# One decoder block on one core: the conditioning vector's load, the first rounded operand, r from PSUM, and the planner's clock

## Chip, core and metric

The kernel runs on one core of one Trainium2 chip. The time is device time of one execution in microseconds, the median of several runs. The profile is of one execution, with its own time.

## What is computed

One decoder block on x (1,024 tokens by 1,024 channels, float32), with a conditioning vector c:

```python
c_act = silu(c)
shift1, scale1, gate1, shift2, scale2, gate2 = split(c_act @ ada_w + ada_b, 6)
h = rmsnorm(x, norm1_g) * (1 + scale1) + shift1
u, v, val, gate = split(h @ w_in + b_in)           # 512 channels each
y_a = gelu(u) * (causal 128x128 mixing of layernorm(gelu(v)) per head)
y_b = silu(groupnorm(causal conv31(val * sigmoid(gate))))
x = x + gate1 * (concat(rmsnorm(y_a), rmsnorm(y_b)) @ w_out)
h2 = rmsnorm(x, norm2_g) * (1 + scale2) + shift2
g, up = split(h2 @ w_ffn_in)                        # 2816 channels each
x = x + gate2 * ((silu(g) * up) @ w_ffn_out)
out = rmsnorm(x, norm_f_g) * (1 + scale_f) + shift_f
```

## The kernel before

The data lie transposed: 128 channels on the partitions, tokens along the free dimension, eight tiles x0 to x7 of 128 x 1024. Tokens are worked in two halves of 512. Every large product is made of three matmuls (`mm3`, `product`): an operand is split into a rounded part (`hi`, type fp32r) and a remainder (`lo`), and hi by hi, lo by hi and hi by lo are summed in PSUM.

The start, which the change touches, goes so. `c_row` (L518) is loaded into one partition, two matmuls against a row of ones (L538) spread it over all partitions into two PSUM banks, and ScalarE's Silu gives `cact` (L539). The eight first halves of x are loaded (L524), squared on ScalarE (L641), and summed over channels by small fp32 matmuls (L648) into a bank; ScalarE takes the square root (L651), VectorE the reciprocal (L652), and matmuls with a selecting column out of the table `colt` (L654) spread the result r over the partitions of the same bank. With `copy=True` ScalarE then copies r into SBUF (L660). The bank is the only one of its tag (`nrm`); later it serves as one of the eight banks of the first projection.

Then a loop over the eight channel blocks k (L718). Two tiles of `ada` (128 x 1024) are loaded per block and multiplied with `cact` on VectorE with a sum over the row (L559), which gives the shift and scale columns (`ccol`); they land in `ypad` tiles, four in turn. A weight block `wk[k]` is loaded, its rounded part is made by ScalarE (L586) and its remainder by VectorE (L587). The block of x is multiplied by r on VectorE (L725), scaled and shifted by ScalarE in place (L726), rounded by ScalarE (L728), and the remainder is taken by VectorE (L729). Then come 24 matmuls of 512 columns into eight banks (L603 to L605). `gain` and the columns of biases come from `colt` (L521), one table of 277 columns.

Most of the order is not that of the program text. The text is emitted once, and `fix_order` (L452) then plans it: `Graph` collects instructions with what each must follow, `forward` is a list schedule over five engines in which `duration` gives each instruction a time and `Clock` keeps when an engine, the port shared by VectorE and GpSimd and the load queue come free, and `backward` gives each instruction the time from it to the end, which is its rank in the next `forward`. After three rounds the plan with the smallest planned end is kept, and its order on every engine, SyncE's loads too, is written into the program. `issue_after(ins)` adds the demand that what is issued on the same engine in its block comes after `ins`. In the plan before, six loads of x stand ahead of the load of c.

Of the kernel before, what the change touches and what calls it, by code (L numbers as in the profile page):

```python
# [15 lines left out]
D = 1024  # L16
# [51 lines left out]
DMA_ISSUE = 0.44  # L68
DMA_AHEAD = 0.5


# [53 lines left out]
def duration(s):  # L125
# [3 lines left out]
    if s.engine == "PE":  # L129
        n, m = s.writes[0].width, s.reads[1].width  # L130
        if not s.reads[0].f32:
            t = n / 512 * 0.2267
        elif n == 128:
            t = {128: 0.219, 32: 0.068}.get(m, 0.109)
        else:
            t = 0.857
        return t, t + 0.176, 0
# [34 lines left out]
class Graph:  # L172


    def __init__(self, instructions, edges, stacked, reusing):
        self.steps = []
        uses, live, tiles, order = {}, {}, {}, {}
        for ins in instructions:
# [3 lines left out]
            for operands, written in ((s.reads, False), (s.writes, True)):  # L182
                for o in operands:
# [17 lines left out]
                    if o.tile.tag and o.space != "DRAM" and o.name not in s.slots:  # L201
                        s.slots.append(o.name)
            self.steps.append(s)
        by_name = {s.ins.name: s for s in self.steps}
# [108 lines left out]
class Clock:  # L313


    def __init__(self):
        self.free = dict.fromkeys(ENGINES, 0.0)
        self.port = self.queue = 0.0
        self.last, self.partial = None, False

    def run(self, s, t):
        if s.dma:
            gap = (TURN_GAP if self.last is False else LOAD_GAP) if s.load else STORE_GAP if self.last else 0.0
            begin = max(t + (LOAD_WAIT if s.load else STORE_WAIT), self.queue + gap)
            self.queue = begin + s.bytes / (LOAD_RATE if s.load else STORE_RATE)
            self.last = s.load
            self.free["SP"] = max(t + DMA_ISSUE, self.queue - LOAD_WAIT - DMA_AHEAD)
            return t, self.queue
        if s.port:
            t = max(t, self.port)  # L330
            self.port = t + s.port
        if s.engine == "PE" and s.partial != self.partial:
            self.partial = s.partial
            t += 0.09 if s.partial else 0.12
        self.free[s.engine] = t + s.issue
        return t, t + s.finish
# [18 lines left out]
def forward(g, rank):  # L355
# [6 lines left out]
    parked = {tag: [] for tag in g.order}  # L362
    slots, clock, table = Slots(g), Clock(), None

# [16 lines left out]
    for _ in range(count):  # L381
# [21 lines left out]
        for n in s.after:  # L403
            need[n] -= 1
            same = g.steps[n].engine == e and not s.dma
            at[n] = max(at[n], (begin + s.issue if e == "PE" else end) if same else end + SIGNAL[e])
            if not need[n]:
                arrive(n)
# [60 lines left out]
def block_kernel(ctx: ExitStack, tc: tile.TileContext, xT, c, ada, cols, vbias, bs, wsp,  # L469
# [48 lines left out]
    c_row = sb.tile([P, D], F32, tag="raw", name="c_row", bufs=N_RAW)  # L518
    nc.sync.dma_start(c_row[0:1, :], c)
    colt = const.tile([P, NCOL], F32, name="colt")  # L520
    nc.sync.dma_start(colt, cols)  # L521
    xs = [const.tile([P, S], F32, name=f"x{k}") for k in range(KD)]
    for k in range(KD):
        nc.sync.dma_start(xs[k][:, hs(0)], xT[k, :, hs(0)])  # L524

# [105 lines left out]
    def rstd(srcs, n, name, groups, add_eng, copy=False, size=H, tmp=tmp, bank=None):  # L631
# [28 lines left out]
        A.activation(r, bank, AF.Copy)  # L660
        return r

# [47 lines left out]

    r1a = rstd(x_half(0), D, "n1_0", (1,) * 8, None, True)
    h1 = [[None] * KD, [None] * KD]
# [5 lines left out]
    for k in range(KD):  # L718
# [5 lines left out]
        t = tmp(f"t_h1_0_{k}")  # L724
        V.tensor_tensor(t, xs[k][:, hs(0)], r1a, op=ALU.mult)  # L725
        A.activation(t, t, AF.Identity, bias=ccol(SHIFT1, k), scale=ccol(SCALE1, k))  # L726
        h = h1[0][k] = act_tile(f"h1_0_{k}", 0)
        A.activation(h[:, 0, :], t, AF.Copy)  # L728
        V.tensor_tensor(h[:, 1, :], t, h[:, 0, :].bitcast(F32), op=ALU.subtract)  # L729
# [686 lines left out]
```

## Time and profile before

| | |
|---|---|
| median of 3 runs | 996.74 us (996.4 to 1000.49) |
| profiled execution | 996.41 us, span 994.4 us |
| mean granted TensorE clock | 0.995 |
| TensorE, VectorE, ScalarE, GpSimd busy | 97%, 86%, 48%, 39% |

The span runs from the first to the last instruction of the profiled execution; the rest of its time lies around it. The busy share of TensorE counts modelled ends of pipelined matmuls, so where its pace is wanted the number of matmuls in a stretch is the better reading.

### The profile page before, as it was taken

What the parts mean: (1) busy time and instruction counts of PE and PEld (TensorE: products, weight loads), DVE (VectorE), ACT (ScalarE), POOL (GpSimd) and SP (SyncE); (2) the same over time, 40 slices, a digit from 0 to 9 for tenths busy, and PEclk for the clock granted to TensorE, in tenths of its full rate; (3) what the DMA queues carried; (4) which work ended last, traced back from release to release, by engine and by line L of the source; (5) the groups of instructions that cost most, each with busy time, mean ns of one, the idle gap of its engine ahead of it and who ended that gap; (6) DMA issues with size and microseconds to landing.
All of it is one profiled execution on the core that took longest, in us unless ns stands there. A gap on an engine that the chain in (4) does not pass through costs nothing.

```text
span 994.4 us, 13218 instructions
## 1 busy us (share of the span) xinstructions
PE 961.9 (97%) x4645; PEld 773.6 (78%) x4645; DVE 855.2 (86%) x1197; ACT 474.0 (48%) x751; POOL 391.4 (39%) x232
## 2 busy tenths in 40 slices
PE   4999999999999999999999999999999999999994
PEld 2887777778878778888888877888887888888873
DVE  3969999999999444799999999998678989869946
ACT  6668467643484363564332332323337437236416
POOL 0037879755556111574445544445443100000121
PEclk9999999999999999999999999999999999999997
DMA  8983351524465515764677777677557838315104
GB/s 301 329 315 101 123 175 56 189 96 127 148 223 180 190 43 169 259 232 145 221 253 233 244 240 255 227 241 234 186 180 259 303 131 259 121 40 173 33 1 169
DMA packets 73667, 184.08 MB, mean 185 GB/s; under 512 B 8193, under 2 KB 10497, under 8 KB 73602
## 3 DMA queue, kind: packets, MB, share of 16 engines
q1 hardware_dynamic: 73602, 183.25, 55.6%
q8 instruction: 36, 0.59, 0.3%
q14 instruction: 29, 0.24, 0.1%
HBM read 142.06 MB, written 41.16 MB: 184 GB/s over the span
## 4 chain that ended last, share of the span: by engine, by line
PE 83%; DVE 10%; issue 2%; ACT 2%; DMA 1%; POOL 0%; SPq 0%; ACTq 0%; DVEq 0%; POOLq 0%
PE B L928 24%; PE C L928 14%; PE ah L928 11%; PE p L603 3%; PE po L603 3%; PE po L604 3%; PE po L605 3%; PE p L604 3%; PE p L605 3%; PE A L928 3%; DVE w_f L921 2%; PE v L604 2%; PE v L603 1%; PE pu L605 1%; PE v L605 1%
## 5 line engine op out<-in xcount | busy, mean ns | idle before, releaser
L928 PE MATMUL B<-h,w_f 128*128 128x512 f32 x816 | 190.8, 390 | 2.3 <-ACT x L1145 1.2
L928 PEld LDWEIGHTS B<-h,w_f 128*128 128x128 f32 x816 | 152.7, 188 | 36.4 <-DVE x L1147 3.1
L866 DVE SCALAR_TENSOR_TENSOR cv<-ypad,colt,cv 128x512 f32<-128x512 f32 x216 | 147.6, 745 | 0.5
L928 PE MATMUL B<-fa,w_d 128*128 128x512 f32 x528 | 125.5, 390 | 0.3 <-DVE x L1277 0.2
L928 PE MATMUL C<-h,w_f 128*128 128x512 f32 x528 | 123.6, 389 | 0.0
L928 PEld LDWEIGHTS B<-fa,w_d 128*128 128x128 f32 x528 | 98.8, 188 | 22.0 <-DVE x L1277 1.1
L928 PEld LDWEIGHTS C<-h,w_f 128*128 128x128 f32 x528 | 99.1, 188 | 20.6
L928 PE MATMUL ah<-h,wh_a 128*128 128x512 f32 x320 | 101.6, 395 | 0.5 <-ACT sg L673 0.5
L1209 POOL TENSOR_TENSOR sq_nf<-sq_nf,sq_nf 128x512 f32<-128x512 f32 x9 | 12.5, 1388 | 175.6 <-ACT sq_nf L1204 175.6
L920 ACT ACTIVATE w_d<-raw_d 128x512 fp32r<-128x512 f32 (+1 forms) x72 | 42.0, 593 | 83.0 <-PE B L928 34.0
L1170 POOL TENSOR_TENSOR x<-x,up 128x512 f32<-128x512 f32 x20 | 34.7, 1737 | 106.1 <-ACT x L1169 106.1
L587 POOL TENSOR_TENSOR wl_a<-raw_a,wh_a 128x1024 fp32r<-128x1024 f32 x20 | 49.2, 2461 | 67.8 <-ACT wh_a L586 57.7
L920 ACT ACTIVATE w_f<-raw_f 128x512 fp32r<-128x512 f32 x68 | 42.3, 627 | 68.4 <-PE B L928 41.6
L921 DVE TENSOR_TENSOR w_f<-raw_f,w_f 128x512 fp32r<-128x512 f32 x68 | 68.7, 1017 | 5.1 <-ACT w_f L920 5.0
L928 PEld LDWEIGHTS ah<-h,wh_a 128*128 128x128 f32 x320 | 59.9, 188 | 15.1 <-issue 1.4
L928 PE MATMUL C<-fa,w_d 128*128 128x512 f32 (+1 forms) x273 | 64.4, 384 | 0.0
L928 PE MATMUL ah<-h,wl_a 128*128 128x512 f32 x160 | 62.2, 390 | 0.0
L928 PEld LDWEIGHTS C<-fa,w_d 128*128 128x128 f32 x273 | 49.9, 188 | 11.0 <-issue 0.8
L921 DVE TENSOR_TENSOR fa<-a,fa 128x512 fp32r<-128x512 f32 x77 | 54.2, 743 | 1.7 <-ACT fa L920 1.7
L1277 DVE SCALAR_TENSOR_TENSOR x<-B,cond,x 128x512 f32<-128x512 f32 x48 | 35.6, 743 | 19.8 <-PE B L928 19.8
L920 ACT ACTIVATE fa<-a 128x512 fp32r<-128x512 f32 x77 | 46.0, 626 | 8.8 <-DMA a<-acts 5.7
L921 DVE TENSOR_TENSOR w_d<-raw_d,w_d 128x512 fp32r<-128x512 f32 (+1 forms) x72 | 47.8, 673 | 1.4 <-ACT w_d L920 1.4
(236 smaller groups left out, 2094.2 us busy)
## 6 DMA issues: line engine op xcount, KB each, us to landing
acts<-x SPq DMA_DIRECT2D x77, 256.0 KB, 3.1
a<-acts SPq DMA_DIRECT2D x77, 256.0 KB, 4.0
raw_f<-wf SPq DMA_DIRECT2D x32, 512.0 KB, 4.5
ada<-ada SPq DMA_DIRECT2D x24, 512.0 KB, 3.4
x<-ada SPq DMA_DIRECT2D x24, 512.0 KB, 3.8
raw_a<-wf SPq DMA_DIRECT2D x20, 512.0 KB, 3.8
ahead<-ahead SPq DMA_DIRECT2D x40, 256.0 KB, 3.0
ypad<-ada SPq DMA_DIRECT2D x16, 512.0 KB, 5.4
```

The lines of the kernel that those rows point to most:

```text
L587: lo_eng.tensor_tensor(lo, raw, hi.bitcast(F32), op=ALU.subtract)
L603: PE.matmul(acc, shi, mhi, start=start, stop=False)
L604: PE.matmul(acc, slo, mhi, start=False, stop=False)
L605: PE.matmul(acc, shi, mlo, start=False, stop=stop)
L866: V.scalar_tensor_tensor(accs[j], src, wc, accs[j], op0=ALU.mult, op1=ALU.add)
L920: A.activation(dst[:, 0, :], src, AF.Copy)
L921: lo_eng.tensor_tensor(dst[:, 1, :], src, dst[:, 0, :].bitcast(F32), op=ALU.subtract)
L928: last_mm = PE.matmul(bank[:, cols], s, m[:, cols], start=first and p == 0 and i == 0, stop=p == n - 1 and i == 2, skip_group_check=True)
L1170: G.tensor_tensor(g0, g0, up0, op=ALU.mult)
L1209: G.tensor_tensor(sums[half], sums[half], t, op=ALU.add)
L1277: V.scalar_tensor_tensor(xs[k][:, part], bank[:, cols], ccol(GATE2, k), xs[k][:, part], op0=ALU.mult, op1=ALU.add)
```

## The change

Four things are changed. The load of c is issued first; the eight loads of x and the load of `colt` must follow it, and `colt` now stands behind x in the text. In the loop over blocks, the rounded operand is made by one ScalarE pass (scale, shift and rounding at once) out of the product with r, and the unrounded value by a second pass over the same product. Block 0 is multiplied by r out of the PSUM bank, the other seven out of the copy. In the planner, small fp32 matmuls get other times, TensorE's writes to one bank keep their order in the text, and the forward plan doubles a matmul's time where the engine was little used shortly before (`tensor`, `throttled`).

```diff
--- before.py
+++ after.py
@@ -67,6 +67,7 @@
 LOAD_GAP, STORE_GAP, TURN_GAP = 0.07, 0.24, 0.3
 DMA_ISSUE = 0.44
 DMA_AHEAD = 0.5
+CLOCK_WINDOW = 3.4133
 
 
 class Step:
@@ -130,10 +131,9 @@
         n, m = s.writes[0].width, s.reads[1].width
         if not s.reads[0].f32:
             t = n / 512 * 0.2267
-        elif n == 128:
-            t = {128: 0.219, 32: 0.068}.get(m, 0.109)
         else:
-            t = 0.857
+            k = s.reads[0].box[1] - s.reads[0].box[0]
+            t = {128: 0.219, 32: 0.068}.get(m, 0.109 if k > 64 else 0.055) * n / 128
         return t, t + 0.176, 0
     if s.engine == "Activation":
         psum = any(o.space == "PSUM" for o in s.reads)
@@ -174,7 +174,7 @@
 
     def __init__(self, instructions, edges, stacked, reusing):
         self.steps = []
-        uses, live, tiles, order = {}, {}, {}, {}
+        uses, live, tiles, order, bank = {}, {}, {}, {}, {}
         for ins in instructions:
             if not type(ins).__name__.startswith("Inst"):
                 continue
@@ -200,6 +200,10 @@
                         uses[o.name].append(s.n)
                     if o.tile.tag and o.space != "DRAM" and o.name not in s.slots:
                         s.slots.append(o.name)
+            if s.engine == "PE":
+                if s.writes[0].name in bank:
+                    s.before.add(bank[s.writes[0].name])
+                bank[s.writes[0].name] = s.n
             self.steps.append(s)
         by_name = {s.ins.name: s for s in self.steps}
         for later, earlier in edges:
@@ -313,10 +317,28 @@
 class Clock:
 
 
-    def __init__(self):
+    def __init__(self, throttled=False):
         self.free = dict.fromkeys(ENGINES, 0.0)
         self.port = self.queue = 0.0
         self.last, self.partial = None, False
+        self.throttled, self.active = throttled, {}
+
+    def tensor(self, t, s):
+
+        if s.partial != self.partial:
+            self.partial = s.partial
+            t += 0.09 if s.partial else 0.12
+        w = int(t / CLOCK_WINDOW)
+        slow = 2 if self.throttled and self.active.get(w - 1, 0.0) < CLOCK_WINDOW / 2 else 1
+        end = t + slow * s.issue
+        a = t
+        while a < end:
+            w = int(a / CLOCK_WINDOW + 1e-9)
+            b = min(end, (w + 1) * CLOCK_WINDOW)
+            self.active[w] = self.active.get(w, 0.0) + b - a
+            a = b
+        self.free["PE"] = end
+        return t, t + slow * s.finish
 
     def run(self, s, t):
         if s.dma:
@@ -329,9 +351,8 @@
         if s.port:
             t = max(t, self.port)
             self.port = t + s.port
-        if s.engine == "PE" and s.partial != self.partial:
-            self.partial = s.partial
-            t += 0.09 if s.partial else 0.12
+        if s.engine == "PE":
+            return self.tensor(t, s)
         self.free[s.engine] = t + s.issue
         return t, t + s.finish
 
@@ -360,7 +381,7 @@
     done, order = [0.0] * count, {e: [] for e in ENGINES}
     ready, waiting = ({e: [] for e in ENGINES} for _ in range(2))
     parked = {tag: [] for tag in g.order}
-    slots, clock, table = Slots(g), Clock(), None
+    slots, clock, table = Slots(g), Clock(True), None
 
     def arrive(n):
         tag, t = slots.blocked_on(g.steps[n])
@@ -403,7 +424,7 @@
         for n in s.after:
             need[n] -= 1
             same = g.steps[n].engine == e and not s.dma
-            at[n] = max(at[n], (begin + s.issue if e == "PE" else end) if same else end + SIGNAL[e])
+            at[n] = max(at[n], (clock.free[e] if e == "PE" else end) if same else end + SIGNAL[e])
             if not need[n]:
                 arrive(n)
     return order, done, slots.follows
@@ -516,12 +537,13 @@
         return slice(half * H, (half + 1) * H)
 
     c_row = sb.tile([P, D], F32, tag="raw", name="c_row", bufs=N_RAW)
-    nc.sync.dma_start(c_row[0:1, :], c)
+    c_load = nc.sync.dma_start(c_row[0:1, :], c).ins
     colt = const.tile([P, NCOL], F32, name="colt")
-    nc.sync.dma_start(colt, cols)
     xs = [const.tile([P, S], F32, name=f"x{k}") for k in range(KD)]
-    for k in range(KD):
-        nc.sync.dma_start(xs[k][:, hs(0)], xT[k, :, hs(0)])
+    with issue_after(c_load):
+        for k in range(KD):
+            nc.sync.dma_start(xs[k][:, hs(0)], xT[k, :, hs(0)])
+        nc.sync.dma_start(colt, cols)
 
     def col(name, i=0):
         o = _OFF[name] + i
@@ -658,7 +680,7 @@
             return bank[:, 0:size]
         r = front.tile([P, H], F32, tag="s", name=f"r_{name}", bufs=4)
         A.activation(r, bank, AF.Copy)
-        return r
+        return bank[:, 0:size], r
 
     def x_half(half):
         return [xs[k][:, hs(half)] for k in range(KD)]
@@ -708,7 +730,7 @@
                                        col("a_ln_b", hp)[rows], bst[rows, hp, :],
                                        op0=ALU.mult, op1=ALU.add)
 
-    r1a = rstd(x_half(0), D, "n1_0", (1,) * 8, None, True)
+    r1a_bank, r1a = rstd(x_half(0), D, "n1_0", (1,) * 8, None, True)
     h1 = [[None] * KD, [None] * KD]
     alloc = [cv_bank] * 2 + [gn_bank] * 2 + [mm_bank] * 3 + [nrm_bank]
     acc = {(j, vg): alloc[2 * j + vg](f"p{j}_{vg}") for j in range(4) for vg in range(2)}
@@ -722,10 +744,10 @@
         A.activation(ccol(SCALE1, k), ccol(SCALE1, k), AF.Identity, bias=gain[:, k:k + 1], scale=col("norm1_g", k))
         A.activation(ccol(SHIFT1, k), ccol(SHIFT1, k), AF.Identity, bias=bcol(SHIFT1, k))
         t = tmp(f"t_h1_0_{k}")
-        V.tensor_tensor(t, xs[k][:, hs(0)], r1a, op=ALU.mult)
+        V.tensor_tensor(t, xs[k][:, hs(0)], r1a_bank if k == 0 else r1a, op=ALU.mult)
+        h = h1[0][k] = act_tile(f"h1_0_{k}", 0)
+        A.activation(h[:, 0, :], t, AF.Identity, bias=ccol(SHIFT1, k), scale=ccol(SCALE1, k))
         A.activation(t, t, AF.Identity, bias=ccol(SHIFT1, k), scale=ccol(SCALE1, k))
-        h = h1[0][k] = act_tile(f"h1_0_{k}", 0)
-        A.activation(h[:, 0, :], t, AF.Copy)
         V.tensor_tensor(h[:, 1, :], t, h[:, 0, :].bitcast(F32), op=ALU.subtract)
         for j in range(4):
             for vg in range(2):
```

## Rows read from the trace of the kernel before

**Rows 1.** The page: engines, busy us, share of the span, instructions.
```profile
PE 961.9 (97%) x4645; PEld 773.6 (78%) x4645; DVE 855.2 (86%) x1197; ACT 474.0 (48%) x751; POOL 391.4 (39%) x232
```

**Rows 2.** Waits of TensorE, 28 to 970 us: total, times, longest; six rows.
```profile
PE po L603 <- ACT y_b L824: 1.5, 1, 1.5
...
PE B L928 <- DVE x L1277: 0.2, 1, 0.2
```

**Rows 3.** Chain of waits over the start: start us, us, what.
```profile
9.87 2.00 PE c L538 x2
...
15.13 1.90 DVE ypad L559 x3
...
21.89 0.81 ACT t_h L726
22.71 0.95 ACT wh_k L586
23.65 0.53 ACT h L728
...
24.22 0.80 PE p L603
25.02 0.43 PE p L604
...
27.98 0.24 PE p L603
```

**Rows 4.** Timeline, 0 to 32 us: start us, us, what, idle before.
```profile
3.60 0.33 SPq L519 DMA_DIRECT2D c_row<-c  x1
...
10.61 1.28 ACT L539 ACT_TABLE_LOAD   x1
...
10.90 0.17 DVE L716 SCALAR_TENSOR_TENSOR gain<-colt 128x8 f32<-128x8 f32 x1 [9.94 <-DMA colt<-cols]
...
11.91 0.60 ACT L539 ACTIVATE cact<-c 128x512 f32<-128x512 f32 x1
...
12.40 0.62 ACT L641 ACTIVATE sq_n<-x 128x512 f32<-128x512 f32 x1
...
16.61 0.35 ACT L651 ACTIVATE rt_n<-ssq_n,epst 128x128 f32<-128x128 f32 x1
...
17.43 0.95 DVE L652 RECIPROCAL rt_n<-rt_n 128x128 f32<-128x128 f32 x1
...
18.43 2.08 PE L654 MATMUL ssq_n<-rt_n,colt 128*128 128x128 f32 x8 [2.95 <-DVE rt_n L652]
...
20.54 0.60 ACT L660 ACTIVATE r_n<-ssq_n 128x512 f32<-128x512 f32 x1 [1.76 <-PE ssq_n L654]
```

**Rows 5.** Windows: busy us (PE, PEld, DVE, ACT, POOL), clock, DMA share, GB/s.
```profile
0.00:9.40 9.40, 2.79 (x36) 0.99 (x40) 0.09 (x2) 4.54 (x7) 0.49 (x8) 1.00 0.71 238
0.00:10.80 10.80, 4.19 (x41) 1.51 (x42) 0.09 (x2) 5.88 (x9) 0.49 (x8) 1.00 0.75 259
...
0.00:13.40 13.40, 6.79 (x51) 2.21 (x52) 0.26 (x3) 8.09 (x11) 0.49 (x8) 1.00 0.80 288
```

**Rows 6.** VectorE's lines by form, 0 to 280 us: busy us, mean ns.
```profile
L725 DVE TENSOR_TENSOR t_h<-x,r_n 128x512 f32<-128x512 f32 x8 | 5.4, 685 | 0.0
...
L904 DVE TENSOR_TENSOR s<-s,gn 128x512 f32<-128x512 f32 x4 | 2.7, 684 | 0.6 <-PE gn L901 0.6
```

**Rows 7.** Timeline of VectorE, 33 to 39 us.
```profile
33.47 1.22 DVE L587 TENSOR_TENSOR wl_k<-raw_k,wh_k 128x1024 fp32r<-128x1024 f32 x1
34.61 1.22 DVE L559 SCALAR_TENSOR_TENSOR ypad<-ypad,cact 128x1024 f32<-128x1024 f32 x1
...
38.10 1.22 DVE L587 TENSOR_TENSOR wl_k<-raw_k,wh_k 128x1024 fp32r<-128x1024 f32 x1
```

**Rows 8.** Windows of the feed-forward pass; columns as in rows 5.
```profile
460.00:540.00 80.00, 80.00 (x354) 66.26 (x353) 79.58 (x107) 29.59 (x49) 35.70 (x21) 1.00 0.70 229
540.00:620.00 80.00, 78.93 (x343) 63.72 (x342) 79.98 (x101) 23.94 (x40) 40.20 (x24) 1.00 0.77 248
```

## The prediction

> **What bounds the kernel now.** I read the page first: TensorE is busy for 97% of the span, VectorE for 86%, nothing else for more than half [rows 1]. A busy share says nothing of where an edit of the first microseconds lands, so I asked next what TensorE waits for after its first projection has begun. Between 28 and 970 us it waits six times, 4.9 us in all [rows 2]. The reader is to see that from there on the kernel is one long stream of matmuls: whatever brings the start of that stream forward should come out at the end, unless another engine then falls behind.
>
> The chain of waits over the start shows what holds that start back [rows 3]. The first projection matmul runs at 24.22. Going back from it: the rounding pass of the first operand (23.65), a weight copy that stood ahead of it on ScalarE (22.71), the scale and shift pass (21.89), VectorE's products with the conditioning vector (15.13), and the two matmuls that spread that vector over the partitions (the first at 9.87, 2.00 us). The timeline has the engines' own order [rows 4]: SyncE issues the vector's load at 3.60, behind six loads of x; the eighth square starts only at 12.40, behind the Silu table and the first half of the activated vector; the square root comes at 16.61, the reciprocal at 17.43. So the chain that sets the start runs through c, and c is late by the place of its load, not by its size.
>
> **What the loads allow.** Counting bytes from time 0, 238 GB/s over 9.4 us are 2,237 KB: c (4), the eight halves of x (262 each) and the columns (142). To 10.8 us it is 2,797 KB, one conditioning tile (524) more; to 13.4 us 3,859 KB, which is both tiles and the first weight block [rows 5]. The gain product, which waited for the columns, starts at 10.90 [rows 4], so a load may be used up to 1.5 us after its bytes have passed. VectorE's first product at 15.13 therefore had its tile from about 11 or 12 on, and was waiting for c alone.
>
> **Edit 1, c first, columns last.** c moves past six issues, from 3.60 to about 0.8; each load of x moves back by one issue, about 0.4 us, and the columns stay where the planner had them, behind x. An x issue late by 0.4 costs nothing as long as the bytes, not the issues, set the landing; without that cover it is 0.4. With c in hand at 3 to 4 us the two spreading matmuls (2.00 each) end by 9 even with some sums between them, and both halves of the activated vector are done before the first conditioning tile lands. What is late next is the norm: last square, its sum, square root, reciprocal. The last x half lands between 9.1 (its bytes) and 10.9 (the columns behind it). On ScalarE eight squares of 0.62, two activations of 0.60 and a table of 1.28 are 7.4 us of work from about 4.1, so the last square ends between 9.7 and 11.6; a second table load (1.28) may follow before the square root. With the sum (0.7) and the root (0.35) the reciprocal starts between 10.8 and 13.4, or 14.5 if VectorE has just begun a product of 1.22 [rows 7]. I take 13.1, near the upper end, because ScalarE is the crowded engine there. Before it was 17.43.
>
> **Edit 2, the rounded operand in one pass.** Before, from reciprocal to first matmul: 24.22 - 17.43 = 6.79 us, namely 1.0 reciprocal, 2.1 spreading r, 0.6 copy of r, 0.7 product, 0.8 scale and shift, 0.95 weight copy, 0.53 rounding, and hops [rows 3, 4]. The one pass ends where the scale and shift pass ended, so 0.53 goes, and with it the gap into which the weight copy had slipped (0.95): 5.3 remain. The other bound is 6.25, if that copy gets in front all the same. The second pass over the same data now scales too, 0.81 instead of 0.6 for each of eight blocks; that lies on ScalarE, 48% busy, and costs about 0.2 on VectorE's remainder only if VectorE is already waiting for it.
>
> **Edit 3, the first block multiplied out of PSUM.** A VectorE product that reads a bank costs 0.684 [rows 6], the one out of the copy 0.685: reading is no dearer. If both read the bank at once, the 0.6 of the copy leaves the path; if the product is held until the copy is done, nothing does. No row has two engines reading one bank at the same time, so I take nothing, and keep 0.6 for the range. The Trainium skill ("PSUM — Partial Sum Buffer", PSUM bank collisions raise a hardware error) says that two engines must not be in the same bank and quadrant at once, two reads included, and that the compiler orders such pairs; by it the product waits and the edit is worth nothing; no row here shows such a pair.
>
> **Edit 4, the planner.** It adds no instruction; it changes the assumed time of fp32 and early matmuls, and orders writes to one bank. Its price is only a different order on every engine. One place bounds it: VectorE is full from 460 to 620, and in the second half of that TensorE gets 343 matmuls where the first half has 354 [rows 8], 11 x 0.226 = 2.5 us lost. A better order can win back about that and part of the 4.9 of [rows 2]; a worse one can lose as much again. I take 0, +-3.
>
> **The sum.** First matmul at 13.1 + 5.3 = 18.4 against 24.22: 5.8 us earlier (3.5 to 8.7, the ends being 14.5 + 6.25 and 10.8 + 4.7). Is the stream then fed? A block takes 24 x 0.226 = 5.4 us on TensorE, 4.63 on VectorE (33.47 to 38.10 [rows 7]) and 1,573 KB, under 5 us at the rate of [rows 5]. VectorE needs about 11 us of work for two blocks, from 11 or 12 on, so 23; TensorE wants the second block at 18.4 + 5.4 + 1.7 = 25.5. That 1.7 is the slow beginning: eight matmuls stand 0.43 apart (25.02), then 0.23 (27.98) [rows 3]; it was there before and I leave it. So 996.41 - 5.8 = 990.6 for the profiled execution, whose span is 994.4; the median of the three runs is 0.3 above it: 990.9.
>
> **The rivals.**
> *The order gives it back* (0.13). The new plan loses 2.5 to 4 us in the stretch where VectorE is full. For it: TensorE arrives earlier there and VectorE has no idle time to offer [rows 8]. Against it: VectorE's own work also starts earlier. 993.5 to 995.
> *The start gains less* (0.09). The stream starts at 18.4 but starves in the second block, or runs slowly for longer: were all 24 matmuls of the first block 0.43 apart, that is 16 x 0.2 = 3.2 more, 994.1. Against it: the same idle stretch lay ahead of the stream before. The Trainium skill ("TensorE: Matmul & The Clock Gate", Part 1) says that the throttled state is the default and that activity releases it, and this change takes the two long fp32 matmuls from just ahead of the stream; no row shows the stream without them.
> *The order gains too* (0.10). The 2.5 us of [rows 8] come back besides: 988 or less.
> *Slower* (0.06). If VectorE sets TensorE's pace through the whole first feed-forward pass, 448 to 745, at the loss rate of [rows 8] (11 of 354, 3.1%), that is 9.2 us, of which 2.5 are paid already: +6.7 - 5.8, 997.6. It decides from 5.8 us of new loss on; at twice the rate, 1007. For it: VectorE is at 100% in both halves of that stretch. Against it: after 620 the waits of [rows 2] are few.
> *Edit 3 does nothing*: already in the sum; the other way it is 990.3.
>
> **How the numbers follow.** The forecast with a gain of 3.5 to 8.7 holds the rest, 0.62: 988 to 993.4 alone. About 0.5% (5 us) is what a measurement of this kernel can tell; the forecast lies 0.9 beyond it. Of its 0.62 I give 0.47 to gains above 5, with 0.10 of the rival that gains: 0.57 faster. The rest of the forecast (0.15), both small rivals (0.22) and some of the slower one make 0.38 within 0.5%; 0.05 slower. The range goes from 986.5 (gain of 7 and an order that wins 3) to 996 (order rival at its end): about 0.16 lies outside.
>
> **What would show it.** c issued ahead of every load of x, its two matmuls over before 9; the reciprocal near 13; the first projection matmul near 18.4, with no whole weight copy or second pass between product and rounded operand; the product of block 0 either beside or behind the copy of r. Then the stream without a wait in its first 40 us, the end of the first projection some 6 us earlier, and the same distance at 280, 448 and 745. A distance that shrinks between 448 and 745 is the order rival; one that is small at 70 already breaks the sum over the start. The forecast is wrong if the reciprocal still comes after 15, or if weights land after the operand.

## The result and the profile after

The changed kernel takes 990.72 us (median of five runs, 988.81 to 991.95), the kernel before took 997.85 beside it (five runs, 996.4 to 1000.78). The ratio is 0.9929, interval 0.9912 to 0.9947: 7.1 us, 0.7%, faster. The profiled execution took 991.28 us, its span is 989.6; that is 5.1 us below the profiled execution of before, which was one of the lowest of its runs. The two traces therefore explain about 5 of the 7 us. Three executions of the whole record are in no ratio and no table: two of 2.5 and 3.5 ms, and the profiled one of the kernel with edit 3 undone, which took 1,081.43 us at a granted clock of 0.846.

The page, with the engines as in [rows 1]:

```profile
PE 960.9 (97%) x4645; PEld 775.1 (78%) x4645; DVE 859.5 (87%) x1197; ACT 474.4 (48%) x750; POOL 397.0 (40%) x232
```

The work is the same but for one ScalarE instruction (750 for 751): one table load less. What moved is the beginning. The timeline of the kernel after, 0 to 26 us, which answers [rows 3, 4]; its line numbers are 21 higher than before's at the loads of c and x and 22 higher behind them:

```profile
0.80 0.35 SPq L540 DMA_DIRECT2D c_row<-c  x1
...
1.21 0.83 SPq L576 DMA_DIRECT2D ypad<-ada  x2
...
2.08 4.58 SPq L545 DMA_DIRECT2D x<-xT  x8
...
6.18 0.60 ACT L561 ACTIVATE cact<-c 128x512 f32<-128x512 f32 x1 [1.11 <-PE c L560]
...
7.32 0.63 ACT L663 ACTIVATE sq_n<-x 128x512 f32<-128x512 f32 x1 [0.54 <-DMA x<-xT]
...
9.37 4.55 ACT L663 ACTIVATE sq_n<-x 128x512 f32<-128x512 f32 x7
...
14.69 0.37 ACT L673 ACTIVATE rt_n<-ssq_n,epst 128x128 f32<-128x128 f32 x1 [0.22 <-PE ssq_n L670]
...
15.09 0.95 DVE L674 RECIPROCAL rt_n<-rt_n 128x128 f32<-128x128 f32 x1 [1.35 <-ACT rt_n L673]
...
16.10 2.08 PE L676 MATMUL ssq_n<-rt_n,colt 128*128 128x128 f32 x8 [1.48 <-DVE rt_n L674]
18.21 0.60 ACT L682 ACTIVATE r_n<-ssq_n 128x512 f32<-128x512 f32 x1 [2.21 <-PE ssq_n L676]
18.84 0.69 DVE L747 TENSOR_TENSOR t_h<-x,ssq_n 128x512 f32<-128x512 f32 x1 [1.58 <-ACT r_n L682]
...
19.57 0.81 ACT L749 ACTIVATE h<-t_h,cond 128x512 fp32r<-128x512 f32 x1 [0.76 <-DVE t_h L747]
...
20.43 0.80 PE L625 MATMUL p<-h,wh_k 128*128 128x512 f32 x1 [2.26 <-ACT h L749]
...
21.03 0.63 PE L626 MATMUL p<-h,wl_k 128*128 128x512 f32 x1
...
25.30 0.58 PE L627 MATMUL p<-h,wh_k 128*128 128x512 f32 x1
25.71 0.40 PE L625 MATMUL p<-h,wh_k 128*128 128x512 f32 x1
```

Read it from the top. c goes first, but what follows it on SyncE is two tiles of `ada`, and only then x. Both halves of the activated vector are done at 6.78, some 6 us earlier than the first of them was before. The first square, at 3.70 before, now waits for x until 7.32, and the last half of x lands at 13.18 (10.51 before). From 9.37 on ScalarE does seven squares without a gap (4.55 us), so the reciprocal starts at 15.09, 2.3 us earlier than before. From there the path is short: spreading, copy, product, one rounding pass, first matmul at 20.43, 3.8 us earlier than before.

How that lead travels to the end (us, read from the timelines of TensorE):

| | before | after | earlier by |
|---|---|---|---|
| first projection matmul starts | 24.22 | 20.43 | 3.8 |
| first projection ends | 69.7 | 66.7 | 3.0 |
| product for u ends | 117.5 | 114.8 | 2.7 |
| h2 @ w_ffn_in, first half, starts (`ah`) | 277.25 | 274.31 | 2.9 |
| the same stage ends | 448.4 | 444.8 | 3.6 |
| h2 @ w_ffn_in, second half, ends (`B`) | 761.2 | 756.4 | 4.8 |
| product with w_ffn_out ends (`C`) | 978.1 | 973.3 | 4.9 |

Behind `C` come only the small matmuls of the closing norm.

TensorE's waits after the start, 28 to 980 us (answers [rows 2]; total, times, longest), the two greatest of seven rows:

```profile
PE B L950 <- DVE x L1169: 2.3, 2, 1.3
PE po L625 <- ACT y_b L846: 1.3, 1, 1.3
```

and the windows of the feed-forward pass (columns as in [rows 5], answer to [rows 8]):

```profile
460.00:540.00 80.00, 80.00 (x354) 66.24 (x354) 79.58 (x105) 26.78 (x43) 36.72 (x23) 1.00 0.69 229
540.00:620.00 80.00, 77.69 (x341) 63.68 (x341) 79.98 (x103) 24.88 (x41) 37.04 (x23) 1.00 0.75 247
```

The stretch where VectorE is full still holds TensorE back: 341 matmuls against 354. Nothing was won there, and no more than two matmuls lost. Matmul against matmul, the lead is 3.6 from 448 to 556, 3.25 from 620 to 751, and 4.8 at the end of `B`. This last step is a wait of the kernel before, at 758.19, that the kernel after does not have (a row of the view of [rows 2]):

```profile
PE B L928 <- ACT x L1145: 1.2, 1, 1.2
```

None of the other kernels in the table below has a wait like it there either, so no single edit removed it; whether every execution of the kernel before has it, its one trace can't say.

### The profile page after: what moved, and what is told of

Same layout as the page of the kernel before. It is cut to its first block, busy times and chain, and to the rows that moved or that the text cites. A ratio compares the mean times of both kernels' runs of the same rounds, so it can differ in the third digit from the quotient of the medians.

```text
span 989.6 us, 13221 instructions
## 1 busy us (share of the span) xinstructions
PE 960.9 (97%) x4645; PEld 775.1 (78%) x4645; DVE 859.5 (87%) x1197; ACT 474.4 (48%) x750; POOL 397.0 (40%) x232
## 4 chain that ended last, share of the span: by engine, by line
PE 77%; DVE 10%; issue 3%; ACT 2%; DMA 1%; POOL 0%; SPq 0%; ACTq 0%; DVEq 0%
PE B L950 25%; PE C L950 14%; PE ah L950 11%; PE A L950 3%; PE po L625 3%; PE po L626 3%; PE po L627 3%; DVE w_f L943 2%; PE v L625 2%; PE v L626 2%; PE v L627 1%; PE p L625 1%; PE p L627 1%; PE p L626 1%; DVE x L581 1%
## 5 line engine op out<-in xcount | busy, mean ns | idle before, releaser
L943 DVE TENSOR_TENSOR w_f<-raw_f,w_f 128x512 fp32r<-128x512 f32 x68 | 65.8, 975 | 5.6 <-ACT w_f L942 5.5
L950 PE MATMUL C<-fa,w_d 128*128 128x512 f32 (+1 forms) x273 | 64.2, 384 | 0.0
```

Of the source, the lines that this page charges most:

```text
L943: lo_eng.tensor_tensor(dst[:, 1, :], src, dst[:, 0, :].bitcast(F32), op=ALU.subtract)
L950: last_mm = PE.matmul(bank[:, cols], s, m[:, cols], start=first and p == 0 and i == 0, stop=p == n - 1 and i == 2, skip_group_check=True)
```

## The experiments

The theory was that the start alone makes the gain, c's place above all; the rival was that the planner's new order makes it. The later runs ask why the start gained less than forecast and whether a still earlier start pays. Each ratio is against runs of the kernel before on the same chip.

| kernel | reciprocal | first matmul | projection ends | u ends | `ah` ends | `B` ends | `C` ends | ratio, interval |
|---|---|---|---|---|---|---|---|---|
| before | 17.4 | 24.2 | 69.7 | 117.5 | 448.4 | 761.2 | 978.1 | |
| after | 15.1 | 20.4 | 66.7 | 114.8 | 444.8 | 756.4 | 973.3 | 0.9929, 0.9912 to 0.9947 |
| c first only | 14.7 | 21.6 | 67.4 | 115.0 | 447.3 | 759.9 | 977.1 | 0.9949, 0.9933 to 0.9966 |
| planner only | 17.9 | 26.1 | 72.7 | 123.6 | 454.1 | 767.3 | 984.7 | 1.0030, 1.0018 to 1.0042 |
| all but the planner | 14.7 | 20.1 | 66.2 | 113.4 | 443.2 | 755.3 | 973.4 | 0.9932, 0.9918 to 0.9946 |
| x straight behind c | 13.8 | 19.2 | 65.9 | 113.8 | 443.7 | 756.3 | 972.6 | 0.9924, 0.9908 to 0.9940 |
| two passes | 14.4 | 19.5 | 65.2 | 113.5 | 445.1 | 756.4 | 974.7 | 0.9954, 0.9939 to 0.9968 |
| copy late | 14.2 | 18.0 | 64.6 | 112.5 | 442.4 | 754.4 | 972.7 | 0.9926, 0.9907 to 0.9945 |
| idle matmuls | 15.0 | 19.9 | 63.7 | 111.8 | 445.2 | 757.1 | 974.9 | 0.9928, 0.9903 to 0.9952 |
| idle matmuls, same order | 14.5 | 19.3 | 64.0 | 113.2 | 443.5 | 757.6 | 974.7 | 0.9952, 0.9939 to 0.9965 |
| idle matmuls, copy late | 14.8 | 19.5 | 64.2 | 112.8 | 442.8 | 753.7 | 970.5 | 0.9935, 0.9922 to 0.9949 |
| idle matmuls, copy late, x behind c | 13.9 | 18.9 | 63.6 | 114.9 | 444.9 | 756.9 | 974.2 | 0.9934, 0.9921 to 0.9947 |
| copy late, x behind c | 14.4 | 19.4 | 65.7 | 113.6 | 443.5 | 756.1 | 973.9 | 0.9931, 0.9912 to 0.9949 |

Single executions differ: eight of these with the same load order have the reciprocal anywhere from 14.2 to 15.1, and a profiled execution may lie some us from its kernel's median. So the columns are read for the place where a distance changes, and the ratios for the verdict.

**c first only.** The kernel before with the load edit and nothing else.

```diff
+    c_load = nc.sync.dma_start(c_row[0:1, :], c).ins
...
+    with issue_after(c_load):
+        for k in range(KD):
+            nc.sync.dma_start(xs[k][:, hs(0)], xT[k, :, hs(0)])
+        nc.sync.dma_start(colt, cols)
```

> The kernel before with edit 1 alone (c issued first, x and the columns after it), planner and operand chain as before. Theory A (the start of the matmul stream carries the gain): the plan puts two conditioning tiles between c and x, so the reciprocal comes near 15.1 as in the changed kernel; from there the old chain of 6.8 us gives the first projection matmul near 21.9 instead of 24.2, and the time falls by about 2 us (ratio 0.998). Rival B (the planner's new costs carry it): no gain beyond 1 us, whatever the first matmul does.

The ratio is 0.9949, some 5 of the 7 us, and more than the 2 us expected. (The execution profiled is the longest of six, 995.24; it loses 1.4 us of its lead between 275 and 448, so its row ends only 1.0 us ahead of before.) From reciprocal to first matmul it takes 6.82, as before (6.79). The timeline of its ScalarE shows why:

```profile
19.23 0.81 ACT L727 ACTIVATE t_h<-t_h,cond 128x512 f32<-128x512 f32 x1 [0.49 <-DVE t_h L726]
19.95 1.04 ACT L587 ACTIVATE wh_k<-raw_k 128x1024 fp32r<-128x1024 f32 x1
20.89 0.61 ACT L729 ACTIVATE h<-t_h 128x512 fp32r<-128x512 f32 x1
```

The weight copy slips between the two passes once more, just as in [rows 3].

**Planner only.** The kernel after with the load, the passes and the product as before.

```diff
-    with issue_after(c_load):
...
-        V.tensor_tensor(t, xs[k][:, hs(0)], r1a_bank if k == 0 else r1a, op=ALU.mult)
-        h = h1[0][k] = act_tile(f"h1_0_{k}", 0)
-        A.activation(h[:, 0, :], t, AF.Identity, bias=ccol(SHIFT1, k), scale=ccol(SCALE1, k))
+        V.tensor_tensor(t, xs[k][:, hs(0)], r1a, op=ALU.mult)
```

> The kernel before with the planner's edits alone. Theory A: c stays behind six loads of x, the first projection matmul stays at 24 +-0.5, and the time differs from before by no more than the 2 us that another order makes. Rival B: 4 to 5 us of the gain are here, with matmuls gained back between 448 and 760.

It is slower, 1.0030, so the rival is out; that is 3 us, where no more than 2 either way was expected of a new order, and the first matmul is 1.9 later. In the trace the loss is there at the end of the first projection (3.0). By the end of u it is 6.1, more than the ratio has: TensorE waits 1.26 at 74.0 and 1.59 at 91.3 there, in one of the longer executions. VectorE's timeline:

```profile
19.30 1.23 DVE L608 TENSOR_TENSOR wl_k<-raw_k,wh_k 128x1024 fp32r<-128x1024 f32 x1 [0.44 <-ACT wh_k L607]
20.44 1.22 DVE L580 SCALAR_TENSOR_TENSOR ypad<-ypad,cact 128x1024 f32<-128x1024 f32 x1
21.58 1.22 DVE L580 SCALAR_TENSOR_TENSOR ypad<-ypad,cact 128x1024 f32<-128x1024 f32 x1
...
22.73 1.89 DVE L746 TENSOR_TENSOR t_h<-x,r_n 128x512 f32<-128x512 f32 x3
```

The copy of r is done at 21.6, but the new order has put a weight remainder and two conditioning products ahead of the product with r, and then has three of these in a row. From reciprocal (17.90) to first matmul (26.07) it takes 8.2 us, 6.8 before.

**All but the planner.** The first three edits, planned by the planner of before.

```diff
-    slots, clock, table = Slots(g), Clock(True), None
+    slots, clock, table = Slots(g), Clock(), None
...
-        if s.engine == "PE":
-            return self.tensor(t, s)
```

> The changed kernel with the old planner (edits 1 to 3 alone). Theory A: first projection matmul near 20.4, 3.8 us ahead of before, and a time 3 to 5 us below before. Rival B: a time within 1.5 us of before, the early start being given back later.

0.9932: within its interval all of the gain. The planner's edits cost 3 us on the old start and are worth nothing that can be measured on the new one. Against "c first only", with the same reciprocal (14.73 and 14.74), the first matmul comes at 20.07 instead of 21.56: 1.5 us for edits 2 and 3, of which the next runs give edit 3 none that can be measured.

**Edit 3 undone, and the copy made late.** Two kernels: block 0 multiplied by the copy again; and the kernel after with the copy of r issued behind the first rounded operand.

```diff
-        V.tensor_tensor(t, xs[k][:, hs(0)], r1a_bank if k == 0 else r1a, op=ALU.mult)
+        V.tensor_tensor(t, xs[k][:, hs(0)], r1a, op=ALU.mult)
```

```diff
-        A.activation(r, bank, AF.Copy)
...
+        hi = A.activation(h[:, 0, :], t, AF.Identity, bias=ccol(SHIFT1, k), scale=ccol(SCALE1, k)).ins
+        if k == 0:
+            edges.append((A.activation(r1a, r1a_bank, AF.Copy).ins.name, hi.name))
```

> The changed kernel with edit 3 undone: block 0 too is multiplied by the copy of r in SBUF. Theory A (the product out of PSUM waits for the copy anyway): the product starts at the same distance behind the copy, the first projection matmul stays at 20.4 +-0.3, and the time differs from the changed kernel only by what another order makes (2 us). Rival B (reading the bank saves the copy): first matmul at 21.0.

> The changed kernel with the copy of r written and planned behind the first product and its rounded operand, so that the product out of PSUM has nothing to wait for but the bank itself. Theory A (edit 3 is worth nothing as it stands because the product is held until the copy is done): first projection matmul 0.6 us ahead of 20.4, at 19.8; end of the first projection 0.3 to 0.6 earlier. Rival B (something else holds the product, the spreading matmuls for instance): first matmul at 20.4 as before, and the second block's product later by the 0.6 of the copy.

Without edit 3 the ratio is 0.9931 (0.9907 to 0.9955), the same as with it. With the copy late the product no longer waits; timeline:

```profile
15.15 1.16 PE L676 MATMUL ssq_n<-rt_n,colt 128*128 128x128 f32 x8 [1.48 <-DVE rt_n L674]
...
16.35 0.69 DVE L746 TENSOR_TENSOR t_h<-x,ssq_n 128x512 f32<-128x512 f32 x1
...
18.70 0.58 ACT L750 ACTIVATE r_n<-ssq_n 128x512 f32<-128x512 f32 x1
```

The spreading ends at 16.31 and the product starts 0.04 later; in the kernel after it started 0.66 behind the spreading and 0.03 behind the copy. So where the copy stands first, the product waits for it, although both only read the bank, and edit 3 as it stands takes nothing off the path; the edge that sends the copy behind the operand is what takes the 0.6 off. At the end of the projection it can't be told from an earlier reciprocal (14.15) and quicker spreading, and in the ratio (0.9926) it cannot be seen.

**Two passes.** The kernel after with edit 2 undone.

```diff
-        h = h1[0][k] = act_tile(f"h1_0_{k}", 0)
-        A.activation(h[:, 0, :], t, AF.Identity, bias=ccol(SHIFT1, k), scale=ccol(SCALE1, k))
         A.activation(t, t, AF.Identity, bias=ccol(SHIFT1, k), scale=ccol(SCALE1, k))
+        h = h1[0][k] = act_tile(f"h1_0_{k}", 0)
+        A.activation(h[:, 0, :], t, AF.Copy)
```

> The changed kernel with edit 2 undone: scale and shift in place, then a rounding pass. Theory A (edit 2 takes one rounding pass off the start and the gap into which a weight copy could slip): first projection matmul 0.5 to 1.5 us later than 20.4, time 0.5 to 1.5 us above the changed kernel, give or take 2 us of order. Rival B (the operand was not what the first matmul waited for): first matmul at 20.4.

0.9954, about 2.5 us above the kernel after, with intervals that overlap. In its profile reciprocal to first matmul takes 5.08 although the spreading took only 1.16 (2.08 in the kernel after); at equal spreading that is 0.66 more than after's 5.34 - 0.92 = 4.42, the second pass (0.63) and nothing else. This plan did not slip the weight copy in. At the end of u this execution is still 1.3 ahead of the kernel after; what it loses, it loses after that, and its order differs there. No run shows which place makes the difference of the ratios.

**x straight behind c.** In the plan, what must follow a load counts from the load's landing. Here it counts from its issue.

```diff
+            if (s.n, n) in g.issued:
+                at[n] = max(at[n], begin + s.issue)
+            else:
+                at[n] = max(at[n], (clock.free[e] if e == "PE" else end) if same else end + SIGNAL[e])
```

> The changed kernel with one more planner edit: what must be issued after a load may be planned once that load is issued, not once it has landed. The plan then has c, the eight halves of x, the columns, and only then the conditioning tiles, which is the order that the prediction assumed. Theory A: the reciprocal comes near 13.1 and the first projection matmul near 18.4, 2 us ahead of the changed kernel, and the time falls by about 2 us against it (about 7 against before in span). Rival B: the first matmul moves and the time does not, beyond the 2 us that another order makes. Rival C (the conditioning tiles become the late thing): the reciprocal comes near 13 but the first operand waits for its shift and scale columns, first matmul at 20 or later.

SyncE now issues c, the eight loads of x, the columns, and then `ada`. Timeline:

```profile
1.21 3.68 SPq L554 DMA_DIRECT2D x<-xT  x8
...
11.37 0.58 ACT L570 ACTIVATE cact<-c 128x512 f32<-128x512 f32 x1
...
12.06 1.28 ACT L573 ACT_TABLE_LOAD   x1
...
13.84 0.95 DVE L683 RECIPROCAL rt_n<-rt_n 128x128 f32<-128x128 f32 x1
...
19.18 0.80 PE L634 MATMUL p<-h,wh_k 128*128 128x512 f32 x1 [2.26 <-ACT h L758]
```

The reciprocal comes 1.25 earlier than in the kernel after, still 0.7 behind the forecast: the last square now starts at 10.84 (13.29 in the kernel after), but a second table load stands between it and the root. Two more kernels with this load order, below, have the reciprocal at 13.88 and 14.40, so the usual gain is smaller than 1.25. Reciprocal to first matmul is 5.34, as after. Of the 1.25 us, 0.8 are left at the end of the projection and 0.7 at the end of `C`; the ratio 0.9924 is the same as after's: the rival of the expectation, that the first matmul moves and the time does not.

**Idle matmuls ahead of the stream.** Eight fp32 matmuls of 128 columns, three behind the sums and five behind the spreading, go into a bank that is free, and their result is unused (the trace records each as two). In the first kernel the planner sees them, in the second, whose edit stands here, it doesn't, so that the order is that of the kernel after.

```diff
+    def spin(count, after):
+        spins[after.name] = [PE.matmul(spin_bank[:, 0:P], cact[:, 0:P], cact[:, 0:P], start=True, stop=True).ins
+                             for _ in range(count)]
```

> The changed kernel with eight fp32 matmuls of 128 columns added that nobody reads, three between the last sum of squares and the matmuls that spread r, five between those and the projection, where TensorE stands idle for 1.5 and 2.3 us. In the changed kernel the first twelve projection matmuls stand 0.43 us apart, in the kernel before nine. Theory A (the idle stretches ahead of the stream keep its first matmuls at the lower level): fewer than six stand 0.43 apart, and the first projection ends 1 us or more earlier. Rival B: the count stays at nine to twelve, the end of the projection stays within 0.4 us of the changed kernel's.

> The changed kernel, its order kept instruction for instruction on every engine, with the same eight idle fp32 matmuls put in (three before the spreading matmuls, five behind them), which the planner does not see. In the run where the planner saw them the first projection ended 2.9 us earlier and 3.2 us were lost again by 275 us. Theory A (the loss was the other order): the projection ends at 63.4 +-0.7 and the lead of 2 to 3 us over the changed kernel is still there at 275 and 445; time 1.5 to 3 us below the changed kernel (ratio to before near 0.990). Rival B (the middle of the kernel is bound by VectorE, which an earlier TensorE only waits for): the lead is gone by 275 with the same order, and the time is that of the changed kernel.

The timeline of TensorE in the second:

```profile
16.88 1.28 PE L657 MATMUL p<-cact 128*128 128x128 f32 x10
19.30 0.50 PE L628 MATMUL p<-h,wh_k 128*128 128x512 f32 x1 [1.14 <-ACT h L761]
19.64 0.40 PE L629 MATMUL p<-h,wl_k 128*128 128x512 f32 x1
19.88 0.40 PE L628 MATMUL p<-h,wh_k 128*128 128x512 f32 x1
```

From the second matmul on they stand 0.23 apart, but for one wait of 0.6 at 21.3 for VectorE's remainder; in the kernel after twelve stand 0.43 apart (20.43 to 25.71), in the kernel before eight [rows 3]. The projection ends 2.7 us earlier than after's, 1.1 of it from the earlier start in this execution. The lead is 1.6 at the end of the product for u, 1.3 at 444, and at the end of the span it is gone: 0.9952. So it was neither another order (every engine's order is after's) nor lost by 275, as the two theories had it. Two places took it. One is a wait of 1.5 at 80.9 for the squares of x's second half (0.2 in the kernel after). The other is in the feed-forward pass; its timeline of TensorE:

```profile
612.62 4.62 PE L962 MATMUL B<-h,w_f 128*128 128x512 f32 x12 [1.76 <-DVE x L1181]
```

and its windows ahead of and behind that wait (columns as in [rows 5]):

```profile
605.00:612.00 7.00, 5.86 (x26) 4.50 (x24) 7.00 (x9) 1.90 (x3) 3.75 (x3) 1.00 0.72 216
612.00:619.00 7.00, 6.38 (x21) 5.12 (x22) 5.76 (x10) 1.26 (x2) 0.00 (x0) 0.76 0.83 281
```

TensorE waits 1.76 for VectorE, and then the granted clock falls: twelve matmuls take 4.46 us (612.62 to 617.08), 1.7 more than at 0.23 each. The stall is paid twice. The first kernel of the two (0.9928) has the same at another place, a wait of 1.55 for ScalarE that ends at 197.5, and then eight matmuls 0.43 apart. The slow beginning is real, it is removed, and the time is not shorter for it.

**Where the lead goes.** Idle matmuls with the copy late; the same with x straight behind c; and that without idle matmuls.

```diff
+            edges.append((A.activation(r1a, r1a_bank, AF.Copy).ins.name, hi.name))
...
+        if copy:
+            spin(SPIN[1], last["rstd"])
...
+            if (s.n, n) in g.issued:
```

> The changed kernel with the copy of r behind the first rounded operand and the eight idle matmuls (unseen by the planner). Theory A: the two gains add, 0.6 of the copy and 2 to 3 of the slow matmuls; the first projection ends at 62 to 63.5 against 66.3, and the time is 2 to 4 us below the changed kernel. Rival B: the projection ends there and the time stays within 1 us of the changed kernel.

> As the run with the late copy and the idle matmuls, and with loads that must follow a load planned from its issue on, so that x comes straight behind c. Theory A: 0.8 to 1.3 us more at the start (reciprocal 13.8 instead of 14.1 to 15.1), first projection ended by 61.5 to 63, time 3 to 5 us below the changed kernel (ratio to before near 0.989). Rival B: the order that this plan gives takes it back, time within 1.5 us of the run before it.

> The kernel after with two edits: the copy of r is issued behind the first rounded operand, so that the first product reads the bank without waiting, and the plan lets what follows a load be issued from that load's issue on, so that the eight loads of x stand straight behind c. Each alone gave 0.9926 and 0.9924 of the time before, the kernel after 0.9929. Theory A (what the start gains beyond some 3 us is given back at the second half's norm and by the order): first projection matmul near 18.0 (0.6 before the 18.6 to 19.2 of the load order alone), end of the first projection between 64 and 65, but the span between 988 and 990 and the ratio between 0.9905 and 0.993, within its interval the same as after. Rival B (the two gains of the start add up and stay): ratio 0.9905 or below and a span below 988, with the distance to the kernel after at the end of the first projection (some 2 us) still there at 444 and at 973.

The three ratios, 0.9935, 0.9934 and 0.9931, are again that of the kernel after: the gains of the start do not add up in the time. From 20.3 us on, these three, "x straight behind c", "copy late" and the second kernel with idle matmuls have the order of the kernel after on every engine: what they lose is lost at waits, not by another plan. In the second of them (the execution profiled is its longest, 992.37) the projection ends 3.1 us earlier than after's, and when the product for u ends nothing is left. TensorE's wait in between:

```profile
PE ssq_n L686 <- ACT sq_n L679: 2.0, 1, 2.0
```

and the timeline of that stretch:

```profile
74.23 7.85 POOL L905 TENSOR_TENSOR s<-s,cp 128x512 f32<-128x512 f32 x5 [1.53 <-ACT cp L904]
...
79.64 0.72 ACT L904 ACTIVATE cp<-ypad,colt 128x512 f32<-128x512 f32 x1 [1.49 <-POOL s L905]
80.27 1.66 ACT L679 ACTIVATE sq_n<-x 128x512 f32<-128x512 f32 x3
80.93 1.47 PE L686 MATMUL ssq_n<-sq_n,ones 128*32 128x128 f32 x24 [1.97 <-ACT sq_n L679]
...
83.24 0.63 PE L638 MATMUL pu<-h,wl_u 128*128 128x512 f32 x1
83.66 0.63 PE L639 MATMUL pu<-h,wh_u 128*128 128x512 f32 x1
```

GpSimd adds the taps of the convolution without a pause (7.85 us for five); ScalarE's next tap waits for it, the squares of the second half of x stand behind that tap in ScalarE's order, and TensorE waits for the squares. Behind the wait eight matmuls stand 0.43 apart (83.24 to 86.22), some 1.5 us more. The first kernel of the three meets no such stall in its profiled execution (its shortest, 988.69) and brings 7.7 us of lead over before to the end of `C`; its median of 991.04 says that this is not the rule. The third (profiled in its longest, 992.05) starts at 19.4 and not at the expected 18.0, since its reciprocal comes at 14.40 and its spreading takes 2.08. It passes the place at 81 and loses 0.9 of its 1.3 us over after between 444 and 756, where TensorE waits 1.49 and 1.18 for VectorE's `x` at 556.7 and 613.2 (after: 1.26 and 1.05, which leaves more than half of the 0.9 without a row). After 756 it loses 0.9 more, most of it at two further waits for VectorE, which are 0.17 and 0.35 in the kernel after; timeline of TensorE:

```profile
830.35 3.02 PE L960 MATMUL B<-fa,w_d 128*128 128x512 f32 x12 [0.79 <-DVE x L1309]
...
847.74 4.16 PE L960 MATMUL B<-fa,w_d 128*128 128x512 f32 x17 [0.55 <-DVE x L1309]
```

## Why the forecast came out right, and where its sum was wrong

The forecast was 990.9 and the time is 990.72, but the sum did not come about in the way that it was made.

- *"c moves past six issues, from 3.60 to about 0.8; each load of x moves back by one issue"*: this step failed. c is at 0.80, but the loads of x moved back by three issues: 1,049 KB of `ada` went ahead of them, about 2.6 us at the 400 GB/s that lie between the windows of [rows 5], and the first square came 3.6 later than before. The last half of x landed at 13.18, where 9.1 to 10.9 was forecast, and the reciprocal came at 15.09, not at 13.1, and outside the bounds given (10.8 to 14.5). Some 0.4 of the 2.0 is this execution: the eight with this load order have it at 14.7 in the middle, still 1.6 late. The prediction took the demand "after c" to mean "straight after c"; the plan counts such a demand from c's landing and fills SyncE's time until then. The three kernels with x straight behind c show it: the last square starts at 10.84 to 11.40 (12.34 to 13.29 in the eight), and the reciprocal comes at 13.84, 13.88 and 14.40, inside those bounds and near their upper end, with the second table load that the prediction had counted as possible. So `ada` ahead of x costs the reciprocal 0.3 to 0.9 against the middle of the eight; the other 0.7 to 1.3 is there with the assumed order too, and has that table load (1.28) in it.
- *Edit 2, 5.3 us from reciprocal to first matmul*: right, 5.34. "c first only" against "all but the planner" gives it back as 6.82 and 5.34, with the weight copy in the gap and without it. That the copy stays out is the plan's doing: in "two passes" it stays out too. And the 5.3 holds for spreading at 2.08; where it took 1.16, the same path took 0.9 less.
- *Edit 3, nothing*: right, by the reason given. The product started 0.66 behind the spreading and 0.03 behind the copy, and "copy late" shows the price of 0.6. The Trainium skill ("PSUM — Partial Sum Buffer", PSUM bank collisions raise a hardware error) says that the compiler's scheduler puts a dependency between any two instructions of different engines on one bank and quadrant, two reads included; the trace agrees (0.03), and no run shows what holds the second reader in this program.
- *Edit 4, 0 within 3*: right for this start; on the old one it costs 3 us. After's distance to before grows from 3.0 at the end of the projection to 4.9 at the end of `C`; that 1.8 is a term which the sum had at zero. It comes in parts (0.9 from the end of u to 448, then 1.2 up to 761: 0.3 lost where VectorE is full, and 1.5 won where the kernel before waits at 758). "All but the planner" has 3.5 at the projection, 5.2 at 448 and 4.7 at the end under the old plan. It belongs to no edit that a run could single out, and stays open.
- *The slow beginning, "it was there before and I leave it"*: mis-sized. Twelve slow matmuls instead of eight cost 4 x 0.2 = 0.8, all of the 0.8 between the lead at the first matmul (3.8) and at the end of the projection (3.0). The rival "the start gains less" had this mechanism and its direction. The Trainium skill ("TensorE: Matmul & The Clock Gate", Part 1) says that the throttled state is the default and that activity releases it; the idle matmuls bear it out, 0.43 apart without them and 0.23 with them.
- *"The same distance at 280, 448 and 745"*: it did not shrink: 2.9, 3.6 and, at 751, 3.25, of the 3 us that came. Kernels with a lead of 5 to 6 us at the end of the projection are no faster by their ratios than after with 3. Where their traces show the loss, it is at waits of 0.7 to 2 us for an engine that is not yet ready, and in three of them the slower clock behind one; which of these places takes how much in the median execution is open.

So 2.0 less at the reciprocal and 0.8 less at the slow beginning, against 1.8 more behind the projection: 5.8 - 2.0 - 0.8 + 1.8 = 4.8, the difference of the spans. The medians differ by 2 us more than the two profiles, since the profiled execution of before was a low one; that part of the agreement is luck. It is luck too that the 1.8, most of it the wait of the kernel before at 758, made up for most of the 2.8 that the start fell short.

## What to carry to other kernels

When an edge to a load is handed to a planner, look at whether it counts from the load's issue or from its landing, and read the issue order on SyncE before costing what stands behind it. Reading a value straight out of a PSUM bank, so as not to wait for its copy, gained nothing until the copy itself was sent behind that read. Before shortening a start further, look for the waits that an earlier stream will run into, and count a stall of TensorE with the slow matmuls that may come behind it: here a lead of 3 us came through, and of what was added to it nothing that could be measured.

## What the hardware showed unexpectedly

- The slow beginning follows idle time ahead of the stream. In "copy late" the spreading runs at the upper level (1.16 us for eight), TensorE then stands from 16.3 to 18.0, and the granted clock falls; its windows:

```profile
14.00:17.00 3.00, 1.16 (x8) 0.97 (x8) 2.82 (x4) 1.06 (x2) 0.00 (x0) 1.00 1.03 412
17.00:24.00 7.00, 6.00 (x14) 4.70 (x15) 6.99 (x12) 6.21 (x10) 0.00 (x0) 0.51 1.03 410
24.00:28.00 4.00, 4.00 (x19) 3.29 (x19) 4.00 (x7) 2.64 (x6) 0.00 (x0) 1.00 0.90 308
```

  0.51 is the 1.2 GHz level, and 0.43 us for 512 columns agrees. In the kernel after the spreading took 2.08 and the level had not risen yet; there the column says 1.00 through the whole slow stretch. Until it shows a first change, the spacing of the matmuls is the better witness.
- A stall inside the stream can cost the clock as well: behind waits of 1.50 ("c first only", at 364), 1.55, 1.76 and 1.97 us seven or eight matmuls ran slow; behind the wait of 1.50 at the same line in the kernel before [rows 2], those of 1.57 there in "all but the planner" and "two passes", one of 1.59 in "planner only", one of 1.49 at 556.7 in the last kernel of the table and those of 1.3 in the kernel after none did. So the length of the wait alone does not decide it; what does was not tried.
- The reciprocal scatters by 0.9 us (14.15 to 15.09) over eight profiled executions whose first loads are issued in the same order. It follows the last half of x, which lands between 12.24 and 13.18: the reciprocal starts 1.68 to 1.91 behind it.
